# Three edits to a decoder trunk: Gate normalized by ScalarE, paired k tiles in the values' units, one low half earlier

## The chip, the cores and the metric

The kernel runs on one core of one Trainium2 chip. The metric is the device time of one execution in microseconds. Before the change the median of 3 runs is 386.59 us (385.78 to 387.56).

## The reference, cut to what matters

One layer of a decoder trunk. The input x (1024 tokens by 1024 channels) is projected once into all branches; three branches are gated, concatenated and projected out, and a LayerNorm closes the layer. The branch that the change touches is the gating MLP, called Gate here:

```python
z = x @ w_in
u_a, v_a, g_a, x_b, g_b, q_x, g_x = split(z)
# Gate: 4 heads of 128 channels, chunks of 128 tokens
vh    = layer_norm(gelu(v_a) per token and head, ln_g, ln_b)
mixed = einsum('hts,bcshd->bcthd', tril(w_s), vh) + b_s
y_a   = gelu(u_a) * mixed * silu(g_a)
# two more branches: a diagonal state-space layer (y_b), attention into 256 memory tokens (y_x)
y   = concat([y_a, y_b * silu(g_b), y_x * silu(g_x)])
out = layer_norm(2**0.25 * x + y @ w_out, ln_g, ln_b)
```

## The kernel before

Large products are made in three passes: an operand is split into a high half (`h_...`, rounded to the matmul's format by a copy, mostly on ScalarE) and a low half (`l_...`, the rest, a subtraction on VectorE), and TensorE adds high*high, high*low and low*high (`mm3`, L142; `mm3x2`, L148). x itself lies transposed and split in `xh` and `xl`, eight k tiles of 128 input channels.

The program runs through these stages: a first stage (L543 to L563) that streams x and the weights of two branches in and multiplies them as they land; keys and values of the memory (`KV`); then a list of *units* (`run_units`, L176), each of which multiplies 128 or 512 output columns by all of x; then the output projection (L1160 on). A feature unit (`fm`, L181) makes 128 features for all tokens in two PSUM banks. A values' unit (`vu`, L198) makes 512 columns of v for 4 token tiles of 128, in four PSUM banks: `for kt` over six k tiles, inside it `for t` over the four token tiles, and then the last two k tiles token tile by token tile, each followed by its evacuation. There are two such units, v0 (tokens 0 to 511) and v1. The order of units is xb0, xb1, gb0, gb1, v0, u0 to u3, v1, g0 to g3. Weights come in pieces of 128x512; high and low halves have 6 buffers each (`NPC`).

Beside the units run jobs written as generators. `tick(cost)` after some matmuls advances a notional clock, and jobs whose time has come put their next instructions into the program. Two kinds matter here:

- `ssm_batch` (L722), four batches of the state-space layer. Each has a step in which TensorE transposes `L` into PSUM (`pp`), ScalarE copies it to SBUF (`PP`, L755), and TensorE multiplies with it (`up`, L780); VectorE then makes a scan and `H` (L787 to L802), and TensorE uses `H` in `yp` (L808). GpSimd makes the tables C, S and Q for the next batch (L743 to L777).
- `mix_all(th)` (L892), once after each values' unit. VectorE makes the variance column `rsv` (L895), GpSimd raises it to the power -0.5 (L896), then each of 16 tiles of 128x128 in `nv` (4 heads, 4 chunks) is normalized by one VectorE instruction with two per-partition columns, mean and 1/std (L902); TensorE mixes them with the masked matrix `wT` (`mx`, L911) and VectorE scales the result into `ya`.

TensorE's instructions stand in the order in which the program text issues them, through the whole kernel. Between the KV stage and the output projection, `ordered("p")` leaves the order on VectorE, ScalarE and GpSimd to a scheduler, which places each instruction by estimated times; each engine then runs its own list strictly in order. In the first stage and in the output projection the text's order stands on those engines too.

In the first stage, k tile 0 is loaded in cuts. The weight's second half (`i == 1`, L510 to L523) is split by VectorE (cast `h_wgq`, subtraction `l_wgq`), and `xl[:, 0, half[1]]`, the low half of x's second 512 tokens, follows it.

Of the kernel before, what the change touches and what calls it, by code (L numbers as in the profile page):

```python
# [9 lines left out]
F32 = mybir.dt.float32  # L10
# [3 lines left out]
AF = mybir.ActivationFunctionType  # L14
ALU = mybir.AluOpType
# [3 lines left out]
P = 128  # L19
KT = 8  # L20
# [16 lines left out]
def trunk_kernel(ctx, tc, xT, x, w_gq, w_kv, memT, w_fm, w_v, w_o,  # L37
# [3 lines left out]
    V, S, G, T = nc.vector, nc.scalar, nc.gpsimd, nc.tensor  # L41
# [13 lines left out]
    def mul(eng, o, a, b):  # L55
        eng.tensor_tensor(o, a, b, op=ALU.mult)
# [4 lines left out]
    def sub(eng, o, a, b):  # L61
        eng.tensor_tensor(o, a, b, op=ALU.subtract)  # L62

    def split(hi, lo, src):
        S.copy(hi, src)  # L65
        sub(V, lo, src, hi.bitcast(F32))

    def open_pool(name, bufs=1, side="left", space=None):
        st = ExitStack()
        kw = dict(name=name, bufs=bufs)  # L70
        if space is not None:
            kw["space"] = space
        else:
            kw["side"] = side
        return st, st.enter_context(tc.tile_pool(**kw))
# [12 lines left out]
    def zbank(name):  # L88
        return psz.tile([P, 512], F32, tag="z", name=name)

    def ubank(name):
        return psu.tile([P, 512], F32, tag="u", name=name)
# [28 lines left out]
    def tick(cost):  # L121
        now[0] += cost
        advance()
# [6 lines left out]
    def load(src, name, shape=(P, 512), pool=None, tag="raw", bufs=NRAW):  # L130
        raw = (pool or stream).tile(list(shape), F32, tag=tag, bufs=bufs, name=f"r_{name}")
        nc.sync.dma_start(out=raw, in_=src)
        return raw

    def piece(src, name):
        raw = load(src, name)
        hi = stream.tile([P, 512], F32R, tag="hi", bufs=NPC, name=f"h_{name}")
        lo = stream.tile([P, 512], F32R, tag="lo", bufs=NPC, name=f"l_{name}")
        split(hi, lo, raw)
        return hi, lo  # L140

    def mm3(ps, sh, sl, mh, ml, start, stop, chk=False):  # L142
        kw = dict(skip_group_check=True) if chk else {}
        T.matmul(ps, lhsT=sh, rhs=mh, start=start, stop=False, **kw)  # L144
        T.matmul(ps, lhsT=sh, rhs=ml, start=False, stop=False, **kw)  # L145
        T.matmul(ps, lhsT=sl, rhs=mh, start=False, stop=stop, **kw)  # L146
# [9 lines left out]
    xh = xpool.tile([P, KT, SEQ], F32R, name="xh")  # L156
    xl = xpool.tile([P, KT, SEQ], F32R, name="xl")
# [4 lines left out]
    half = [slice(0, 512), slice(512, 1024)]  # L162
# [35 lines left out]
    def vu(h, evac, done):  # L198


        def run(u, nxt):
            ps = [zbank(f"zv{h}{t}") for t in range(4)]

            def mm(t, kt):
                ts = slice((4 * h + t) * P, (4 * h + t) * P + P)
                mm3(ps[t], xh[:, kt, ts], xl[:, kt, ts], *u.pcs[kt], kt == 0, kt == KT - 1)

            for kt in range(KT - 2):
                u.fetch(kt + 4)
                for t in range(4):  # L210
                    mm(t, kt)
                    if t % 2:
                        tick(1.36)
            for t in range(4):
                for kt in (KT - 2, KT - 1):
                    mm(t, kt)
                evac(t, ps[t])
                if t == 3:
                    done()
                tick(1.36)  # L220
                if t in (1, 2) and nxt is not None:
                    nxt.fetch(t)
        return Unit(f"v{h}", lambda i: w_v[:, i], KT, run, 4)
# [275 lines left out]
    def stage(kt):  # L499
        if kt == 0:  # L500
            ws, xs = [], []
            for i, (a, b) in enumerate(cuts):
                ws.append(load(w_gq[:, kt, a:b], f"wgq0{i}", shape=(P, 256)))
                if i == 0:
                    xs = [load(xT[:, kt, c:d], f"x0{c}", shape=(P, 256), pool=mpool, tag="xraw",
                               bufs=NXR) for c, d in cuts]
                    r1 = load(xT[:, kt, half[1]], "x01")
            wt = []
            for i, raw in enumerate(ws):
                wh = stream.tile([P, 256], F32R, tag="hi", bufs=NPC, name=f"h_wgq0{i}")  # L510
                wl = stream.tile([P, 256], F32R, tag="lo", bufs=NPC, name=f"l_wgq0{i}")
                V.tensor_copy(wh, raw)
                if i == 0:
                    for r, (c, d) in zip(xs, cuts):
                        S.copy(xh[:, 0, c:d], r)
                sub(V, wl, raw, wh.bitcast(F32))
                if i == 0:
                    for r, (c, d) in zip(xs, cuts):
                        sub(V, xl[:, 0, c:d], r, xh[:, 0, c:d].bitcast(F32))
                    S.copy(xh[:, 0, half[1]], r1)  # L520
                else:
                    sub(V, xl[:, 0, half[1]], r1, xh[:, 0, half[1]].bitcast(F32))
                wt += [(wh[:, 0:P], wl[:, 0:P]), (wh[:, P:256], wl[:, P:256])]  # L523
        else:
            wh, wl = piece(w_gq[:, kt], f"wgq{kt}")
            for h in range(2):
                split(xh[:, kt, half[h]], xl[:, kt, half[h]],
                      load(xT[:, kt, half[h]], f"x{kt}{h}", pool=mpool, tag="xraw", bufs=NXR))
            wt = [(wh[:, tok[f]], wl[:, tok[f]]) for f in range(4)]
        return wt  # L530

    def first_half(wt):
# [7 lines left out]
        for w, x in ((0, 0), (0, 1), (1, 0)):  # L540
            mm(1, w, x, 0, 512, w + x == 0)

    wts = [stage(0)]  # L543
    for kt in range(KT):
        wt = wts[kt]
        if kt < KT - 1:
            wts.append(stage(kt + 1))
        if kt == KT - 1:
            kv.fetch(1)
        for f in range(4):  # L550
            wh, wl = wt[f]
            if kt == 0 and f < 2:
                if f == 0:
                    first_half(wt)
                mm3(fps[f][1], wh, wl, xh[:, 0, half[1]], xl[:, 0, half[1]], True, False)
            else:
                mm3x2(fps[f], wh, wl, kt, kt == 0, kt == KT - 1,
                      skip=(0,) if f < 2 else ())
            if kt == KT - 1 and f < 2:
                for h in range(2):  # L560
                    S.activation(yx[:, f, half[h]], fps[f][h], AF.Silu)
        if kt < KT - 1:
            tick(5.2)  # L563
# [136 lines left out]
    gb0 = fm(0, "gb0", raw_to(yb, 0))  # L700
    gb1 = fm(1, "gb1", raw_to(yb, 1))
    v_units = [vu(h, lambda t, ps, h=h: v_evac(h, t, ps), lambda h=h: v_done(h)) for h in range(2)]
    run_units([*xb, gb0, gb1], v_units[0])
    drain()
# [7 lines left out]
    gm_st, gm = open_pool("gm", side="right")  # L712
# [176 lines left out]
    def v_done(th):  # L889
        spawn(mix_all(th))  # L890

    def mix_all(th):  # L892
        v = nv[th]
        _, mv, rs = stt[th]
        V.tensor_scalar(rs, mv[:, :, 1], LN_EPS, None, op0=ALU.add)  # L895
        G.tensor_tensor(rs, rs, nhalf, op=ALU.pow)  # L896
        yield 5.0
        for hd in range(4):
            for c in range(4):
                i = c * 4 + hd  # L900
                sl = v[:, c, tok[hd]]
                V.tensor_scalar(sl, sl, mv[:, i, 0:1], rs[:, i:i + 1], op0=ALU.subtract,  # L902
                                op1=ALU.mult)
            yield 1.0
        yield 4.0
        for hd in range(4):
            while hd not in have_u:
                yield 1.0
            ps = ubank(f"mx{hd}{th}")
            for c in range(4):  # L910
                T.matmul(ps[:, tok[c]], lhsT=v[:, c, tok[hd]], rhs=wT[:, hd],  # L911
                         start=(c == 0), stop=(c == 3), skip_group_check=True)
            now[0] += 0.85
            mt = gm.tile([P, 4, P], F32, tag="mt", bufs=2, name=f"mt{hd}{th}")
            V.scalar_tensor_tensor(mt, ps.rearrange("p (c t) -> p c t", c=4),
                                   gmg[:, hd:hd + 1],
                                   tbias[:, hd].unsqueeze(1).to_broadcast([P, 4, P]),
                                   op0=ALU.mult, op1=ALU.add)
            mul(V, ya[:, hd, half[th]], ya[:, hd, half[th]], mt.rearrange("p c t -> p (c t)"))
            yield 2.0  # L920
# [395 lines left out]
```

## Time and profile before

| what | value |
|---|---|
| runs | 386.59 us median of 3 (385.78 to 387.56) |
| the profiled execution | 383.81 us, its span 382.1 us |
| TensorE busy | 367.4 us (96%) |
| VectorE busy | 293.8 us (77%) |
| ScalarE busy | 181.5 us (48%) |
| GpSimd busy | 96.7 us (25%) |
| mean granted TensorE clock | 0.989 |

The profile is of one execution. A timeline row gives start and length in microseconds, the engine (PE is TensorE, DVE VectorE, ACT ScalarE, POOL GpSimd), the line, the operation, the tile written and the tiles read, and in square brackets the time that the engine stood idle just before and what ended it. Ends of matmuls are modelled, so what a stop costs is best read from start to start.

### The profile page before, as it was taken

How to read it: one execution, taken by the hardware profiler on the slowest of the kernel's cores; microseconds unless marked ns; L12 is line 12 of the kernel's file. 1: busy time of each engine (PE TensorE's matmuls, PEld its weight loads, DVE VectorE, ACT ScalarE, POOL GpSimd, SP SyncE). 2: the span in 40 equal slices, each digit the busy share in tenths (PEclk: the TensorE clock that was granted, in tenths of full speed). 3: DMA queues.
4: the chain of work that ended last, by engine and by line, in shares of the span. 5: the costliest groups of instructions: out<-in, count | busy, mean ns of one | idle time of the engine just before them, and what ended most of it. 6: DMA issues, size and time to landing. Idle time of an engine off the chain costs nothing.

```text
span 382.1 us, 5532 instructions
## 1 busy us (share of the span) xinstructions
PE 367.4 (96%) x1877; PEld 310.0 (81%) x1877; DVE 293.8 (77%) x639; ACT 181.5 (48%) x349; POOL 96.7 (25%) x87
## 2 busy tenths in 40 slices
PE   8999999999999999999999999999999999999980
PEld 7888898888888788888888888888888888877870
DVE  4699897988886599969788459775538997777783
ACT  4573597567774635232132334333424667545430
POOL 1305000001000593860873800500000022003541
PEclk9999999999999999999999999999999999999995
DMA  7984436237899776202212232400107959820988
GB/s 221 302 274 124 131 112 192 86 98 206 171 188 235 189 196 162 60 29 58 69 41 60 55 95 62 165 2 0 57 4 214 380 152 225 208 84 0 256 224 235
DMA packets 28628, 53.69 MB, mean 141 GB/s; under 512 B 5928, under 2 KB 9400, under 8 KB 27448
## 3 DMA queue, kind: packets, MB, share of 16 engines
q1 hardware_dynamic: 26296, 44.43, 38.0%
q0 software_dynamic: 2160, 8.39, 11.8%
q10 hardware_dynamic: 144, 0.52, 0.4%
q8 instruction: 15, 0.25, 0.3%
q14 instruction: 13, 0.11, 0.1%
HBM read 44.87 MB, written 13.63 MB: 153 GB/s over the span
## 4 chain that ended last, share of the span: by engine, by line
PE 67%; DVE 19%; issue 4%; ACT 4%; DMA 3%; POOL 1%; SPq 0%; POOLq 0%; DVEq 0%; ACTq 0%
PE zg L151 4%; PE zg L152 4%; PE zg L154 4%; PE zv L144 3%; PE zv L146 3%; PE zv L145 3%; PE av L624 2%; PE zxb L152 2%; PE zxb L154 2%; PE zxb L151 2%; PE q L152 2%; PE q L154 2%; PE q L151 2%; DVE l_u L62 2%; DMA r_wo<-in_w_o_dram 2%
## 5 line engine op out<-in xcount | busy, mean ns | idle before, releaser
L144 PE MATMUL zv<-h_v,xh 128*128 128x512 f32 x64 | 25.6, 400 | 0.3 <-ACT yb L229 0.3
L151 PE MATMUL zu<-xh,h_u 128*128 128x512 f32 x64 | 25.9, 404 | 0.0
L151 PE MATMUL zg<-xh,h_g 128*128 128x512 f32 x64 | 25.5, 398 | 0.0
L152 PE MATMUL zu<-xl,h_u 128*128 128x512 f32 x64 | 25.0, 391 | 0.0
L152 PE MATMUL zg<-xl,h_g 128*128 128x512 f32 x64 | 25.0, 390 | 0.0
L146 PE MATMUL zv<-h_v,xl 128*128 128x512 f32 x64 | 25.0, 390 | 0.0
L145 PE MATMUL zv<-l_v,xh 128*128 128x512 f32 x64 | 24.9, 389 | 0.0
L1029 POOL DMA_DIRECT2D l_wo<-ws_s x6 | 5.2, 863 | 72.8 <-ACT l_wo L1028 66.0
L65 ACT CAST h_v<-r_v 128x512 fp32r<-128x512 f32 x16 | 9.9, 619 | 26.5 <-PE zu L152 18.6
L62 DVE TENSOR_TENSOR l_v<-r_v,h_v 128x512 fp32r<-128x512 f32 x16 | 16.7, 1050 | 6.3 <-ACT h_v L65 6.2
L154 PE MATMUL zu<-xh,l_u 128*128 128x512 f32 x64 | 19.8, 390 | 0.0
L154 PE MATMUL zg<-xh,l_g 128*128 128x512 f32 x64 | 19.7, 390 | 0.0
L596 ACT ACTIVATE pr<-s,nm 128x256 f32<-128x256 f32 x32 | 14.9, 473 | 7.9 <-DVE nm L592 6.5
L1072 POOL TENSOR_TENSOR stat<-stat,nhalf 128x1 f32<-128x1 f32 x7 | 10.3, 1466 | 24.1 <-DVE stat L1071 24.1
L1066 ACT ACTIVATE junk<-res,stat 128x1024 bf16<-128x1024 f32 x7 | 8.1, 1150 | 16.6 <-DVE stat L1062 15.2
L902 DVE TENSOR_SCALAR nv<-nv,mv,rsv 128x128 f32<-128x128 f32 x32 | 13.3, 487 | 3.0 <-POOL rsv L896 3.0
L144 PEld LDWEIGHTS zv<-h_v,xh 128*128 128x128 f32 x64 | 12.0, 188 | 3.0 <-ACT yb L229 0.7
L62 DVE TENSOR_TENSOR l_wo<-r_wo,h_wo 128x512 fp32r<-128x512 f32 x18 | 12.1, 686 | 2.7 <-ACT h_wo L65 2.7
L154 PEld LDWEIGHTS zu<-xh,l_u 128*128 128x128 f32 x64 | 12.0, 188 | 2.6
L146 PEld LDWEIGHTS zv<-h_v,xl 128*128 128x128 f32 x64 | 12.0, 188 | 2.6
L154 PEld LDWEIGHTS zg<-xh,l_g 128*128 128x128 f32 x64 | 12.0, 188 | 2.6
L151 PEld LDWEIGHTS zg<-xh,h_g 128*128 128x128 f32 x64 | 12.0, 188 | 2.3
(371 smaller groups left out, 1187.2 us busy)
## 6 DMA issues: line engine op xcount, KB each, us to landing
r_v<-in_w_v_dram SPq DMA_DIRECT2D x16, 256.0 KB, 2.9
ws_s<-in_w_o_dram SPq DMA_DIRECT2D x4, 1024.0 KB, 6.2
r_wo<-ws_s SPq DMA_DIRECT2D x16, 256.0 KB, 3.4
res<-in_x_dram SPq DMA_DIRECT2D x4, 1024.0 KB, 11.7
r_x<-in_xT_dram SPq DMA_DIRECT2D x15, 256.0 KB, 4.5
r_wo<-in_w_o_dram SPq DMA_DIRECT2D x12, 256.0 KB, 4.4
out_dram<-res SPq DMA_DIRECT2D x6, 512.0 KB, 4.0
res<-lnp POOLq DMA_DIRECT2D x5, 512.0 KB, 4.6
```

The lines of the kernel that those rows point to most:

```text
L62: eng.tensor_tensor(o, a, b, op=ALU.subtract)
L65: S.copy(hi, src)
L144: T.matmul(ps, lhsT=sh, rhs=mh, start=start, stop=False, **kw)
L145: T.matmul(ps, lhsT=sh, rhs=ml, start=False, stop=False, **kw)
L146: T.matmul(ps, lhsT=sl, rhs=mh, start=False, stop=stop, **kw)
L151: T.matmul(ps[h], lhsT=wh, rhs=xh[:, kt, half[h]], start=first, stop=False, **kw[h])
L152: T.matmul(ps[h], lhsT=wh, rhs=xl[:, kt, half[h]], start=False, stop=False, **kw[h])
L154: T.matmul(ps[h], lhsT=wl, rhs=xh[:, kt, half[h]], start=False, stop=last, **kw[h])
L596: S.activation(pr[:, h], ps3[:, h], AF.Exp, bias=nm[:, h:h + 1], scale=1.0, accum_out=rs[:, h:h + 1])
L902: V.tensor_scalar(sl, sl, mv[:, i, 0:1], rs[:, i:i + 1], op0=ALU.subtract, op1=ALU.mult)
L1066: S.activation(junk, res[:, t], AF.Square, bias=nmean[:, i1], scale=1.0, accum_out=ssq[:, i1])
L1072: G.tensor_tensor(rsd[:, i], rsd[:, i], nhalf[:, 0:n], op=ALU.pow)
```

## The change

Three edits. In a values' unit two k tiles are multiplied for token tiles 0 and 1, and then the same two k tiles for token tiles 2 and 3; the calls that fetch pieces and the ticks keep their places. In the first stage `xl[:, 0, half[1]]` is made right after the cast of the weight's second half, ahead of that weight's low half. In `mix_all` VectorE makes one more column, nb = -mean/std, and the 16 tiles are normalized by ScalarE, as Identity(scale * v + nb) with 1/std as the scale, in place of the 16 VectorE instructions.

```diff
     def vu(h, evac, done):
...
-            for kt in range(KT - 2):
-                u.fetch(kt + 4)
-                for t in range(4):
-                    mm(t, kt)
-                    if t % 2:
+            for k0 in range(0, KT - 2, 2):
+                for t0 in (0, 2):
+                    u.fetch(k0 + 4 + t0 // 2)
+                    for kt in (k0, k0 + 1):
+                        for t in (t0, t0 + 1):
+                            mm(t, kt)
                         tick(1.36)
...
                 V.tensor_copy(wh, raw)
+                if i == 1:
+                    sub(V, xl[:, 0, half[1]], r1, xh[:, 0, half[1]].bitcast(F32))
...
-                else:
-                    sub(V, xl[:, 0, half[1]], r1, xh[:, 0, half[1]].bitcast(F32))
...
         G.tensor_tensor(rs, rs, nhalf, op=ALU.pow)
+        nb = gm.tile([P, 16], F32, tag="nbv", name=f"nbv{th}")
+        V.scalar_tensor_tensor(nb, mv[:, :, 0], -1.0, rs, op0=ALU.mult, op1=ALU.mult)
         yield 5.0
         for hd in range(4):
             for c in range(4):
                 i = c * 4 + hd
                 sl = v[:, c, tok[hd]]
-                V.tensor_scalar(sl, sl, mv[:, i, 0:1], rs[:, i:i + 1], op0=ALU.subtract,
-                                op1=ALU.mult)
+                S.activation(sl, sl, AF.Identity, bias=nb[:, i:i + 1], scale=rs[:, i:i + 1])
```

The scheduler gives the instructions these places. On ScalarE, behind v0, before (numbers in names are buffers; `zu` is a u unit's PSUM, `pp` and `up` are the second batch's of `ssm_batch`):

```order
L814 ACTIVATE ytok_1909<-yp_1900 128x4x8x16
L65 CAST h_u_0_2173<-r_u_0_2171 128x512
L755 COPY PP_1984<-pp_1979 128x512
L65 CAST h_u_1_2197<-r_u_1_2195 128x512
L926 ACTIVATE ya<-zu_1886 128x512
L926 ACTIVATE ya<-zu_1887 128x512
L785 COPY ju_2045<-up_2038 64x512
```

and in the change:

```order
L816 ACTIVATE ytok_1911<-yp_1902 128x4x8x16
L65 CAST h_u_0_2175<-r_u_0_2173 128x512
L906 ACTIVATE nv_1810<-nv_1810,nbv_1886,rsv_1813 128x128 x16
L757 COPY PP_1986<-pp_1981 128x512
L65 CAST h_u_1_2199<-r_u_1_2197 128x512
L929 ACTIVATE ya<-zu_1888 128x512
L929 ACTIVATE ya<-zu_1889 128x512
L787 COPY ju_2047<-up_2040 64x512
```

All 16 activations of v0 stand between a cast and the copy of PP, and everything behind them keeps its order. Behind v1 the other 16 stand between two casts of `yth` and the table load ahead of g0's Silu; no table load is added on either place.

On VectorE at the same place, before:

```order
L887 BN_AGGR mv_1812<-stt_1811 128x2 x4
L895 TENSOR_SCALAR rsv_1813<-mv_1812 128x16
L902 TENSOR_SCALAR nv_1810<-nv_1810,mv_1812,rsv_1813 128x128 x16
L62 TENSOR_TENSOR l_u_0_2174<-r_u_0_2171,h_u_0_2173 128x512
L765 COPY K_1991<-kp_1986 128x16 x4
L56 TENSOR_TENSOR L_2153<-Fr,B_145 128x512
```

and in the change:

```order
L889 BN_AGGR mv_1812<-stt_1811 128x2 x4
L897 TENSOR_SCALAR rsv_1813<-mv_1812 128x16
L900 SCALAR_TENSOR_TENSOR nbv_1886<-mv_1812,rsv_1813 128x16
L62 TENSOR_TENSOR l_u_0_2176<-r_u_0_2173,h_u_0_2175 128x512
L767 COPY K_1993<-kp_1988 128x16 x4
L56 TENSOR_TENSOR L_2155<-Fr,B_145 128x512
```

The small nb has the place of the 16. GpSimd's list is the same in both, with Q of the next batch right behind the power.

On VectorE in the batch that leads to the first `yp`, one subtraction `l_u` moves from ahead of `jg` to behind the first product of `H`; before:

```order
L793 SCALAR_TENSOR_TENSOR t_1758<-r_155,v_1757 128x128 x4
L62 TENSOR_TENSOR l_u_0_1935<-r_u_0_1932,h_u_0_1934 128x512
L796 TENSOR_SCALAR jg_1794<-t_1758 64x512
L797 COPY jg_1794<-t_1758 64x512
L56 TENSOR_TENSOR H_1795<-C_1647,t_1758 128x4x127
L56 TENSOR_TENSOR jg_1794<-S_1648,jg_1794 128x512
L62 TENSOR_TENSOR l_u_1_1952<-r_u_1_1949,h_u_1_1951 128x512
L59 TENSOR_TENSOR H_1795<-H_1795,jg_1794 128x4x127
```

and in the change:

```order
L795 SCALAR_TENSOR_TENSOR t_1758<-r_155,v_1757 128x128 x4
L798 TENSOR_SCALAR jg_1794<-t_1758 64x512
L799 COPY jg_1794<-t_1758 64x512
L56 TENSOR_TENSOR H_1795<-C_1647,t_1758 128x4x127
L62 TENSOR_TENSOR l_u_0_1937<-r_u_0_1934,h_u_0_1936 128x512
L56 TENSOR_TENSOR jg_1794<-S_1648,jg_1794 128x512
L62 TENSOR_TENSOR l_u_1_1954<-r_u_1_1951,h_u_1_1953 128x512
L59 TENSOR_TENSOR H_1795<-H_1795,jg_1794 128x4x127
```

As many instructions stand ahead of the last one as before. TensorE's list differs in the two values' units alone.

## Rows read from the trace of the kernel before

**Rows 1.** The page: busy time of each engine.
```profile
PE 367.4 (96%) x1877; PEld 310.0 (81%) x1877; DVE 293.8 (77%) x639; ACT 181.5 (48%) x349; POOL 96.7 (25%) x87
```
**Rows 2.** Timeline of TensorE, its stops and the matmul before three of them.
```profile
7.04 0.50 PE L145 MATMUL gx<-xl,h_wgq 128*128 128x512 f32 x1 [0.47 <-DVE xl L62]
...
129.03 0.39 PE L146 MATMUL zv<-h_v,xl 128*128 128x512 f32 x1
129.75 0.50 PE L144 MATMUL zv<-h_v,xh 128*128 128x512 f32 x1 [0.32 <-ACT yb L229]
...
155.35 0.39 PE L806 MATMUL yp<-M,X 128*128 128x128 f32 x2
156.15 0.46 PE L808 MATMUL yp<-Q,H 128*128 128x128 f32 x2 [0.41 <-DVE H L59]
...
183.72 0.39 PE L806 MATMUL yp<-M,X 128*128 128x128 f32 x2
184.64 0.46 PE L808 MATMUL yp<-Q,H 128*128 128x128 f32 x2 [0.54 <-DVE H L59]
...
342.14 0.50 PE L144 MATMUL o<-h_wo,T4h 128*128 128x512 f32 x1 [0.48 <-DVE res L1101]
```
**Rows 3.** Timeline of VectorE, first stage.
```profile
5.96 0.42 DVE L62 TENSOR_TENSOR l_wgq<-r_wgq,h_wgq 128x256 fp32r<-128x256 f32 x1
6.30 0.68 DVE L62 TENSOR_TENSOR xl<-r_x,xh 128x512 fp32r<-128x512 f32 x1
```
**Rows 4.** Window: length, then PE, PEld, DVE, ACT, POOL busy, PEclk, DMA share, GB/s.
```profile
129.60:162.30 32.70, 32.15 (x158) 26.95 (x159) 32.41 (x66) 13.07 (x22) 24.90 (x20) 1.00 0.59 154
```
**Rows 5.** Timeline of VectorE and GpSimd around both power and K.
```profile
139.95 1.62 POOL L59 TENSOR_TENSOR S<-S,t 128x512 f32<-128x512 f32 x1
140.35 1.30 DVE L59 TENSOR_TENSOR K<-K,ddiag 16x64 f32<-16x64 f32 x1
...
162.36 2.93 POOL L896 TENSOR_TENSOR rsv<-rsv,nhalf 128x16 f32<-128x16 f32 x1 [1.23 <-DVE rsv L895]
165.27 1.05 POOL L56 TENSOR_TENSOR Q<-wr,Cc 128x512 f32<-128x512 f32 x1
165.32 6.95 DVE L902 TENSOR_SCALAR nv<-nv,mv,rsv 128x128 f32<-128x128 f32 x16 [3.04 <-POOL rsv L896]
173.72 0.20 DVE L59 TENSOR_TENSOR K<-K,ddiag 16x64 f32<-16x64 f32 x1
```
**Rows 6.** Timeline of ScalarE and TensorE around PP and up.
```profile
163.95 0.59 ACT L755 COPY PP<-pp 128x512 f32<-128x512 f32 x1 [3.03 <-PE pp L753]
167.62 1.08 ACT L926 ACTIVATE ya<-zu 128x512 f32<-128x512 f32 x2
170.06 1.05 PE L780 MATMUL up<-X,PP 128*128 128x128 f32 x8
```
**Rows 7.** Groups of ScalarE by line and shape: busy us, mean ns, idle before.
```profile
L65 ACT CAST xh<-r_x 128x512 fp32r<-128x512 f32 x14 | 8.6, 620 | 3.2 <-DMA r_x<-in_xT_dram 2.8
L934 ACT ACTIVATE sg<-zg 128x512 f32<-128x512 f32 x8 | 4.4, 596 | 13.2 <-PE zg L154 13.2
L848 ACT ACTIVATE sgl<-gl,glub 128x512 f32<-128x512 f32 x4 | 2.7, 687 | 8.9 <-PE gl L146 8.9
L515 ACT CAST xh<-r_x 128x256 fp32r<-128x256 f32 x2 | 0.8, 405 | 1.5 <-DMA r_x<-in_xT_dram 1.4
```
**Rows 8.** Timeline of ScalarE behind v1.
```profile
249.80 1.09 ACT L934 ACTIVATE sg<-zg 128x512 f32<-128x512 f32 x2 [2.36 <-PE zg L154]
```
**Rows 9.** TensorE's first matmuls and its last; the window behind it, as in rows 4.
```profile
1.09 3.17 PE L243 MATMUL warm<-warm 128*128 128x128 bf16 x28 [1.09 <-DVE warm L240]
...
4.79 0.61 PE L534 MATMUL gx<-xh,l_wgq 128*128 128x256 f32 x2
...
370.67 0.28 PE L146 MATMUL o2last<-yx_wo,B21l 128*128 128x256 f32 x1
...
374.00:378.00 4.00, 0.00 (x0) 0.00 (x0) 1.54 (x3) 0.00 (x0) 0.39 (x1) 0.50 1.02 275
```

## Prediction

> **What bounds the kernel now.** I read the page first, then TensorE's timeline for its stops, then the rows of the engines that end each stop. The page gives TensorE 367.4 us of busy time, 96% of the span [rows 1]: the kernel is bound by TensorE's own list, and a change in another engine counts only where TensorE stops, or is made to stop. The timeline shows few stops [rows 2]. At 7.04 TensorE waits for `xl`, at 129.75 for a PSUM bank that ScalarE empties, at 156.15 and at 184.64 for VectorE's `H`. The one at 342.14 lies in the output projection, follows from work that starts behind the last unit, and has no part in the change. So the most that the three edits can give back is the first four.
>
> Read from start to start, their price is this. Matmuls of 512 columns stand about 0.23 us apart; between 129.03 and 129.75 lie 0.72, so 0.49 are lost, and some 0.1 more while the pipe fills again (the matmul behind the stop takes 0.50, its neighbour 0.39). Between 155.35 and 156.15 lie 0.80 where two matmuls of 128 columns take 0.23 (`up` shows eight in 1.05, with the last one's tail [rows 6]): 0.57 lost. At 183.72 to 184.64 it is 0.92 less 0.23: 0.69 lost [rows 2].
>
> The second thing to see is VectorE between 129.60 and 162.30: busy for 32.41 of 32.70 us [rows 4]. In that stretch VectorE sets the time of `H`, and of the variance column behind it; TensorE arriving earlier does not make them earlier.
>
> **The change part by part.**
>
> *x's low half ahead of the weight's.* VectorE makes `l_wgq` from 5.96 and `xl` from 6.30 to 6.98, and TensorE resumes at 7.04 [rows 2, 3]. With the two exchanged, `xl` starts at 5.96: 0.34 earlier. The weight's low half then starts at about 6.6 and ends at 7.0; it is first read by the third feature tile, which TensorE reaches six matmuls, 1.4 us, after the stop. Everything up to v0 runs behind TensorE, so all of it moves by 0.34, VectorE's full stretch too.
>
> *Two k tiles for two token tiles.* The third and fourth bank of v0 are first written behind four groups of three matmuls, not two: 12 x 0.23 = 2.7 us after the unit's start instead of 1.4. The wait at 129.75 was one third of a microsecond, so it goes, and TensorE gains 0.6. The second k tile's piece is needed 1.4 us earlier; pieces 0 to 3 are fetched during the unit before, so I cost this at nothing. A piece's buffer comes free 1.4 us later for every second k tile; the casts that wait for it belong to pieces at least four k tiles ahead, 4 x 2.7 us of cover. But the gain does not last: 26 us later `H` decides, and it has moved by 0.34 only. The moved `l_u` changes nothing there: the same instructions stand ahead of the last one of `H`. So at 156 the stop grows from 0.57 to some 1.2 us, and the net gain is 0.3.
>
> *The 16 activations behind v0.* This is the term that decides. GpSimd's power ends at 162.36 + 2.93 = 165.29, now 164.99. VectorE's nb reads two SBUF operands, and GpSimd starts Q right behind the power [rows 5]. How such a pair runs is seen at 140.35: K, 16x64 with two inputs, took 1.30 us and ended when GpSimd's S (139.95 + 1.62) ended; the same K with GpSimd at rest took 0.20 [rows 5]. So I let nb end with Q, at 165.27 + 1.05 + 0.1 - 0.3 = 166.1. Bounds: 165.2 if it isn't held; 166.1 as taken.
>
> Then 16 activations of 128x128. No row has one. ScalarE's copies from SBUF take 620 ns for 512 columns and 405 for 256, so 0.84 ns a column, and 297 ns for 128; an activation with a per-partition bias takes 687 where one without takes 596 (both from PSUM), 91 more [rows 7]. Two columns (bias and scale) make 297 + 182 = 479. Neighbours overlap by 0.1: two activations of 0.59 took 1.08 [rows 6]. So 15 x 0.38 + 0.48 = 6.2 us. Bounds: 15 x 0.2 + 0.3 = 3.3 with columns free, 16 x 0.48 = 7.7 without overlap. I take 6.2, since both extra prices are read from this engine. ScalarE ends them at 166.15 + 6.2 = 172.35.
>
> Behind them in ScalarE's list stands the copy of PP, which ran at 163.95 before, 6.1 us ahead of the `up` at 170.06 that reads it [rows 6]. That cover is gone: PP starts at 172.3 and ends at 172.9, `up` starts at 173.0 instead of 170.06. TensorE stands for some 2.9 us, and is 2.9 us late behind it. Also queued behind PP are a cast, u0's evacuation (its banks are needed a unit later) and `ju`, whose delay VectorE can take, as follows.
>
> The Trainium skill (ScalarE: Activation LUTs, Rules for kernel authors) says that adding and multiplying belong on VectorE rather than ScalarE. By that rule alone the block would be longer than VectorE's; here VectorE took 6.95 us for the same 16 [rows 5], so by length the move costs nothing, and the loss that I forecast is one of place.
>
> *VectorE without its 16.* It loses 6.95 us behind v0 and gains nb, 0.2 to 1.1. Between the power and the second `yp` VectorE had been full; now it waits for `ju` (some 2.9 us late, with TensorE) and has 3 us to spare. The stop at 184.64 goes: 0.69 back.
>
> *The 16 behind v1.* There ScalarE had been idle for 2.36 us ahead of g0's Silu [rows 8]; 6.2 us more delay that Silu by some 4. Its two banks are wanted again by g2, one unit (48 x 0.23 = 11 us) later. `mx` needs one head's four tiles at a time. I cost this at nothing.
>
> **The sum.** Net at `up`: +2.9 (the first edit's 0.34 is in it); behind 184: -0.7. That is +2.2. Against the profiled execution: 383.81 + 2.2 = 386.0. That execution lies 2.8 below the median of the runs shown, so the forecast as a median is 386.59 + 2.2 = 388.8 us, 0.6% slower.
>
> **The rivals.**
>
> *A. The block is covered (not slower).* If PP is written by 169.7, TensorE never stops there. It takes nb unheld (-0.9) and activations no slower than 0.23 apart (-2.3). For it: VectorE's list relieved, and an engine with 48% load [rows 1]. Against it: the prices of rows 7. Then only gains are left, 0.3 + 0.7: 385.6.
>
> *B. nb is not held by GpSimd.* Against it stands K at 140.35; for it, that the operands are 16 columns. The stop shrinks by 0.9: 387.9.
>
> *C. The granted clock falls in the stop.* TensorE's last matmul ends at 370.95, and the window from 374.00 has a clock of 0.50, 1.2 GHz, against 1.00 before: a pause of some 3 us was enough there [rows 9]. At the start TensorE ran at that level from 1.09 at least until 4.8 (28 matmuls of 128 columns 0.11 apart; 256 columns 0.2 apart [rows 9]), so a fall costs about half of 3.7 us: 388.8 + 1.9 = 390.7. The forecast stop is 2.9, on the edge; against it, shorter stops left the clock at 1.00 [rows 4]. The Trainium skill (TensorE: Matmul & The Clock Gate, Part 1) says that the slow clock is the default and returns after idle time; the tail agrees.
>
> *D. All four stops go and no new one comes:* 0.34 + 0.6 + 0.57 + 0.69 = 2.2 back, 384.4. It needs `H` to be earlier at 156, which full VectorE speaks against.
>
> **How the numbers follow.** Forecast 0.52, A 0.13, B 0.15, C 0.14, D 0.06. The forecast alone spreads over 387.6 to 390.2 (the block's price and the runs' scatter). About 0.5%, 1.93 us, is what a measurement of this kernel can tell from no change: slower begins at 388.52, faster below 384.66. Two thirds of the forecast and all of C are slower, with a little of B: 0.50. D is faster: 0.06. The rest, 0.44, lies between. For 8 in 10 the range leaves out D, the lower half of A and the upper end of C: 385.6 to 391.0.
>
> **What would show it.** Right: TensorE's stop at 7 near 0.1, none at the start of v0, a longer one at the first `yp`, a new one of 2 to 3 us ahead of `up` ended by ScalarE's PP, none at the second `yp`. VectorE some 12 us less busy, ScalarE about 12 more. Wrong: PP done before `up` (A), nb of 0.2 us next to a busy GpSimd (B), a clock below 1.00 between 170 and 180 (C), or a stop behind v1.

## The result: 388.69 us against 386.18, and the profile after

| what | before | after |
|---|---|---|
| median of 20 runs each | 386.18 us (384.84 to 388.24) | 388.69 us (386.36 to 391.67) |
| ratio, 95% interval | | 1.0064 [1.0046, 1.0082] |
| the profiled execution, its span | 383.81, 382.1 us | 387.51, 385.8 us |

The change makes the kernel 0.64% slower. The forecast was 388.8 us, with slower as the likeliest side. Here and below a ratio and its interval come from the runs within 1.5% of a kernel's fastest, so a ratio need not be the quotient of the two medians beside it. Line numbers behind the first edits are higher by 2 to 4 than in [rows 1 to 9].

The page's row of busy times, after:

```profile
PE 366.6 (95%) x1877; PEld 310.3 (80%) x1877; DVE 285.3 (74%) x609; ACT 193.8 (50%) x381; POOL 97.1 (25%) x87
```

Against [rows 1] VectorE is 8.5 us less busy, where some 12 was forecast, and ScalarE 12.3 more, as forecast; TensorE has the same work. TensorE's timeline, after, shows where it stands now; the columns are those of [rows 2]:

```profile
7.45 0.50 PE L145 MATMUL gx<-xl,h_wgq 128*128 128x512 f32 x1 [0.18 <-DVE xl L62]
...
133.53 0.39 PE L146 MATMUL zv<-h_v,xl 128*128 128x512 f32 x1
135.41 0.63 PE L755 MATMUL pp<-ident,L 128*128 128x128 f32 x4 [1.49 <-issue]
...
158.66 0.46 PE L810 MATMUL yp<-Q,H 128*128 128x128 f32 x2 [1.51 <-DVE H L59]
...
175.59 1.16 PE L782 MATMUL up<-X,PP 128*128 128x128 f32 x8 [2.85 <-ACT PP L757]
...
189.53 0.39 PE L810 MATMUL yp<-Q,H 128*128 128x128 f32 x2
...
346.14 0.50 PE L144 MATMUL o<-h_wo,T4h 128*128 128x512 f32 x1 [0.68 <-DVE res L1104]
```

Against [rows 2]: the stop in v0 at 129.75 is gone, and so is the second yp's. The first yp's grew from 0.41 to 1.51. Two are new: 2.85 us ahead of `up`, ended by PP as forecast, and 1.49 us ahead of `pp`, which the prediction does not have. From start to start TensorE is, against before, 0.42 late where v0 starts, 1.42 at `pp`, 2.52 behind the first yp, 5.53 at the second batch's `up`, 4.81 behind the second yp, and 3.72 at the end. The medians differ by 2.5; the two profiles differ by 1.2 more. The stop ahead of `pp` can account for about 1 of that: before's profiled execution has none, and the experiments show that it belongs to none of the edits.

The 1.1 that TensorE wins back between the second yp and the end is in no term of the prediction. Most of it lies in the output projection. Its matmuls with `T1`, the first and the last of 48, before and then after:

```profile
302.92 0.40 PE L144 MATMUL o<-h_wo,T1h 128*128 128x512 f32 x1
...
313.89 0.39 PE L146 MATMUL o<-h_wo,T1l 128*128 128x512 f32 x1
```
```profile
307.22 0.39 PE L144 MATMUL o<-h_wo,T1h 128*128 128x512 f32 x1
...
317.87 0.39 PE L146 MATMUL o<-h_wo,T1l 128*128 128x512 f32 x1
```

They take 10.97 us before and 10.65 after, at a granted clock of 1.00 in both. The same two times, to a hundredth, stand in the profiles of all the experiments below: counting these two, 10.97 in each of the six kernels in which VectorE normalizes the 16 tiles, 10.65 in each of the eight in which ScalarE does. Over the projection's 336 matmuls (231 against 228 ns apart, stops left out) that is about 1.2 us in favour of the ScalarE edit. Why is open: the edit also adds a tile, nb, so other tiles may lie elsewhere in memory, and no run tests that.

The timelines of VectorE, GpSimd and ScalarE, after, around the new stop ahead of `up`:

```profile
164.71 2.92 POOL L898 TENSOR_TENSOR rsv<-rsv,nhalf 128x16 f32<-128x16 f32 x1 [2.77 <-DVE rsv L897]
167.62 1.05 POOL L56 TENSOR_TENSOR Q<-wr,Cc 128x512 f32<-128x512 f32 x1
```
```profile
167.67 1.03 DVE L900 SCALAR_TENSOR_TENSOR nbv<-mv,rsv 128x16 f32<-128x16 f32 x1 [3.04 <-POOL rsv L898]
...
249.56 0.19 DVE L900 SCALAR_TENSOR_TENSOR nbv<-mv,rsv 128x16 f32<-128x16 f32 x1
```
```profile
168.80 6.27 ACT L906 ACTIVATE nv<-nv,nbv,rsv 128x128 f32<-128x128 f32 x16 [5.40 <-DVE nbv L900]
174.98 0.56 ACT L757 COPY PP<-pp 128x512 f32<-128x512 f32 x1
175.44 0.61 ACT L65 CAST h_u<-r_u 128x512 fp32r<-128x512 f32 x1
175.96 1.06 ACT L929 ACTIVATE ya<-zu 128x512 f32<-128x512 f32 x2
177.05 0.58 ACT L787 COPY ju<-up 64x512 f32<-64x512 f32 x1
```

The chain is the one forecast: power, nb until Q's end, 16 activations in 6.27 us, PP, `up`. nb of v0 takes 1.03 us beside Q, nb of v1 0.19 with GpSimd at rest.

**A correction to the part on the change.** It says that GpSimd's list is the same in both. It is not: the paired k tiles also move one instruction there. In the batch behind the first `H`, the subtraction C<-C,t now stands ahead of the product S<-sn,cn. (Further on they also exchange a cast and an activation on ScalarE and a few instructions on VectorE.) Before, in GpSimd's list, and then its timeline after:

```order
L56 TENSOR_TENSOR C_1916<-cn 128x512
L56 TENSOR_TENSOR S_1917<-sn,cn 128x512
L62 TENSOR_TENSOR C_1916<-C_1916,t_1918 128x512
```
```profile
153.34 1.45 POOL L56 TENSOR_TENSOR C<-cn 128x512 f32<-128x512 f32 x1 [1.53 <-DVE H L56]
154.87 1.62 POOL L62 TENSOR_TENSOR C<-C,t 128x512 f32<-128x512 f32 x1
156.46 1.51 POOL L56 TENSOR_TENSOR S<-sn,cn 128x512 f32<-128x512 f32 x1
```

E6 below puts that back alone.

### The profile page after: what moved, and what is told of

Read it like the earlier page. It is cut to its first block, busy times and chain, and to the rows that moved or that the text cites. A ratio compares the mean times of both kernels' runs of the same rounds, so it can differ in the third digit from the quotient of the medians.

```text
span 385.8 us, 5534 instructions
## 1 busy us (share of the span) xinstructions
PE 366.6 (95%) x1877; PEld 310.3 (80%) x1877; DVE 285.3 (74%) x609; ACT 193.8 (50%) x381; POOL 97.1 (25%) x87
## 4 chain that ended last, share of the span: by engine, by line
PE 71%; DVE 13%; ACT 5%; DMA 4%; issue 3%; POOL 1%; SPq 0%; POOLq 0%; DVEq 0%; ACTq 0%
PE zg L151 4%; PE zg L152 4%; PE zg L154 4%; PE zv L146 3%; PE zv L144 3%; PE zv L145 3%; PE zu L151 3%; PE zu L152 3%; PE zu L154 3%; PE av L626 2%; PE zgb L154 2%; PE zgb L152 2%; PE zxb L152 2%; PE zxb L154 2%; PE zgb L151 2%
## 5 line engine op out<-in xcount | busy, mean ns | idle before, releaser
L62 DVE TENSOR_TENSOR l_v<-r_v,h_v 128x512 fp32r<-128x512 f32 x16 | 15.9, 998 | 10.7 <-ACT h_v L65 10.6
L56 DVE TENSOR_TENSOR ya<-ya,sg 128x512 f32<-128x512 f32 x8 | 5.2, 687 | 15.7 <-ACT sg L937 15.7
L906 ACT ACTIVATE nv<-nv,nbv,rsv 128x128 f32<-128x128 f32 x32 | 12.5, 480 | 5.4 <-DVE nbv L900 5.4
L65 ACT CAST h_wo<-r_wo 128x512 fp32r<-128x512 f32 x18 | 10.9, 618 | 6.2 <-DMA r_wo<-ws_s 4.1
```

Of the source, the lines that this page charges most:

```text
L906: S.activation(sl, sl, AF.Identity, bias=nb[:, i:i + 1], scale=rs[:, i:i + 1])
```

## Experiments

Each ratio is against runs of the kernel before on the same chip, taken beside them. E1 to e4 ran on one chip, e5 to e8 on a second, e9 to e12 on a third, so differences between these groups are less sure than those within one.

**One part at a time (e1 to e4).** E1 is the third hunk alone (x's low half), e2 the first hunk alone (paired k tiles), e3 the last hunk alone (ScalarE and nb), e4 the first two edits without ScalarE:

E1, and e4 with e2's lines:

```diff
+                if i == 1:
+                    sub(V, xl[:, 0, half[1]], r1, xh[:, 0, half[1]].bitcast(F32))
...
-                else:
-                    sub(V, xl[:, 0, half[1]], r1, xh[:, 0, half[1]].bitcast(F32))
```

> Only x's low half is made ahead of the weight's; everything else as before. By the forecast's step TensorE's stop near 7 us shrinks from 0.47 to about 0.1, every milestone up to the last stop before the output projection moves by 0.34, and the time falls by 0.3 (about 386 us where before is 386.3). Rival: it gives nothing, since the weight's second half, whose cast stands ahead of both, lands when it lands, and a stop of some 0.2 to 0.5 us stays; time unchanged, and nothing to see beyond the scatter of the landing.

E2:

```diff
-            for kt in range(KT - 2):
...
+            for k0 in range(0, KT - 2, 2):
+                for t0 in (0, 2):
...
```

> Only the paired k tiles in the values' units, with the places that the scheduler then gives (one subtraction of a weight's low half moved on VectorE, GpSimd's C minus t ahead of the product S). By the forecast's step the stop at v0's third bank goes (0.6 gained), and the gain is lost again at the first yp, whose H is not earlier: time unchanged, within 0.3. Theory formed from the trace of the change: with GpSimd's list in the new order three instead of two of VectorE's operations there are held by GpSimd's, H is about 0.9 later than the shorter lead allows, the stop at the first yp is 1.4 to 1.6, and the time is 0.3 to 0.9 longer than before. Rival: the gain is kept, 0.6 shorter.

E3:

```diff
+        V.scalar_tensor_tensor(nb, mv[:, :, 0], -1.0, rs, op0=ALU.mult, op1=ALU.mult)
...
-                V.tensor_scalar(sl, sl, mv[:, i, 0:1], rs[:, i:i + 1], op0=ALU.subtract,
-                                op1=ALU.mult)
+                S.activation(sl, sl, AF.Identity, bias=nb[:, i:i + 1], scale=rs[:, i:i + 1])
```

> Only the 16 tiles moved to ScalarE, with nb. Theory (place): the copy of PP behind the 16 makes a stop ahead of up of 2.9 to 3.2 us, the second yp stop (0.7) goes, time 2.2 to 2.6 longer than before (1.006 to 1.007). Rival (the block's extra instructions or the clock cost everywhere): the stop at up is under 2, and the rest of the loss lies elsewhere. Rival (most of the loss of the whole change comes from the first two edits): under 1 us longer.

> The first two edits without the third. Theory: no stop at up; stop near 7 us smaller, none at v0's third bank, 1.4 to 1.6 at the first yp; the time is within 0.6 of before, and 2 to 3 below the whole change. Rival (what the whole change loses it loses before up): 1 us or more slower than before.

| kernel | median (range, runs) | ratio, 95% interval |
|---|---|---|
| before | 385.56 (382.65 to 389.14, 31) | |
| e1, x's low half | 385.75 (384.08 to 388.33, 12) | 1.0017 [0.9989, 1.0046] |
| e2, paired k tiles | 386.42 (382.73 to 388.16, 12) | 1.0023 [0.9993, 1.0054] |
| e3, ScalarE | 389.21 (387.24 to 390.61, 8) | 1.009 [1.0054, 1.0125] |
| e4, e1 and e2 | 387.32 (382.37 to 388.06, 12) | 1.0027 [0.9994, 1.0061] |

The ScalarE edit alone is slower by as much as the whole change or more: 3.6 us, where 2.2 to 2.6 was expected. The other two, alone or together, can't be told from before; e4's interval leaves room for a loss of 2.4 us. E3's stops on TensorE's timeline:

```profile
136.02 0.63 PE L753 MATMUL pp<-ident,L 128*128 128x128 f32 x4 [2.00 <-issue]
...
158.16 0.46 PE L808 MATMUL yp<-Q,H 128*128 128x128 f32 x2 [0.41 <-DVE H L59]
...
175.26 1.16 PE L780 MATMUL up<-X,PP 128*128 128x128 f32 x8 [2.99 <-ACT PP L755]
```

The stop of 2.9 to 3.2 ahead of `up` is there, and the rival that saw most of the loss in the first two edits falls. Behind that stop the granted clock, 1.00 before it, fell to 0.50, which is 1.2 GHz, and TensorE lost another 1.7 us from start to start before it was back at 1.00. The same happened in e6 below, where it lost 1.5. E3's window, then e6's, columns as in [rows 4]:

```profile
177.00:180.00 3.00, 3.00 (x13) 2.63 (x12) 1.29 (x2) 0.90 (x2) 0.00 (x0) 0.50 0.35 98
```
```profile
176.00:179.00 3.00, 3.00 (x10) 2.42 (x10) 1.29 (x2) 1.36 (x3) 0.00 (x0) 0.50 0.40 108
```

That is rival C of the prediction. How many of e3's 8 runs have it is not shown, nor how much it adds to their 3.6 us.

E3 also has a stop of 2.00 ahead of `pp`, though it changes nothing ahead of that place. E2 has one of 2.21, e4 of 1.85, e1 of 0.32, before none. So this stop belongs to none of the edits. At the first yp e4 has the 1.49 that was expected; e2 has none, because its clock fell to 0.50 behind the stop ahead of `pp` and TensorE came 1.5 later. In every one of these profiles VectorE's first product for `L` waits for the same thing, a transfer of 32 bytes from `ot` (L636, L666). VectorE's timeline, of before, of after and of e3, and GpSimd's of before:

```profile
129.62 0.69 DVE L56 TENSOR_TENSOR L<-Fr,B 128x512 f32<-128x512 f32 x1 [2.15 <-DMA ws_s<-ot]
```
```profile
127.45 0.42 DVE L56 TENSOR_TENSOR yx<-yx,ot 128x256 f32<-128x256 f32 x1
131.05 0.69 DVE L56 TENSOR_TENSOR L<-Fr,B 128x512 f32<-128x512 f32 x1 [3.17 <-DMA ws_s<-ot]
```
```profile
131.67 0.69 DVE L56 TENSOR_TENSOR L<-Fr,B 128x512 f32<-128x512 f32 x1 [4.29 <-DMA ws_s<-ot]
```
```profile
129.63 0.99 POOL L719 MEMSET M<- 128x512 f32 x2 [2.83 <-DMA ws_s<-ot]
```

`L` reads nothing of that transfer, and the memset of `M`, which waits for it too, reads nothing at all. If they wait all the same, the reason is likely to be memory: both belong to a pool opened (L713) behind the closing of the attention stage's pool (L705), and may lie where `ot` lies, which the transfer still reads. E7 tests whether the reading of `ot` is what they wait for.

**One instruction moved (e5, e6).** E5 is the whole change with the second batch's PP copied by VectorE; e6 is the whole change with GpSimd's S back ahead of C minus t in that batch. In both, the lists of all engines are otherwise as in the change:

```diff
-        S.copy(PP, pps.rearrange("p (g q) -> p g q", g=NG))
+        (V.tensor_copy if bi in (1,) else S.copy)(PP, pps.rearrange("p (g q) -> p g q", g=NG))
```

```diff
+            sm = G.tensor_tensor(v4(Sn), sa, cb, op=ALU.mult)
+            with tc.issue_after(sm.ins):
+                sub(G, C, C, t1)
```

> The whole change, but the second batch's copy of PP is VectorE's instead of ScalarE's: one instruction leaves its place behind the 16 activations, all else keeps its order. Theory (the loss is one of place): the stop ahead of up goes or falls under 0.3, since VectorE has nothing to do there; of the 2.85 us some part may return at the second yp, because ju still stands behind the 16 on ScalarE: time 2 to 2.9 below the whole change, 386 to 386.7. Rival (length: whatever waits for ScalarE's block waits all the same): the stop moves on to the second yp with 2 us or more, time 388 or above. Rival (the loss was made ahead of up, by the late L and the first yp): time unchanged.

> The whole change, with GpSimd's product S put back ahead of its subtraction C minus t, as before. Theory (GpSimd's new order holds three of VectorE's operations ahead of the first H instead of two): jg, l_u and H are held twice, not three times, H ends about 0.5 to 1.0 earlier against pp, and the stop at the first yp falls from 1.5 to 0.5 to 1.0, the time by as much. Rival (the stop at the first yp is set by when L is ready and by what VectorE has to do, not by the order on GpSimd): 1.4 to 1.6 again, or whatever the wait ahead of pp leaves of it; time unchanged.

| kernel | median (range, runs) | ratio, 95% interval |
|---|---|---|
| before | 385.58 (382.23 to 388.25, 22) | |
| e5, PP on VectorE | 385.58 (384.69 to 388.0, 12) | 1.0019 [0.9992, 1.0045] |
| e6, S ahead of C minus t | 388.52 (387.57 to 390.18, 10) | 1.0074 [1.0045, 1.0102] |

E5's block on ScalarE is as long as in after, and TensorE passes `up` without a stop:

```profile
167.66 6.28 ACT L905 ACTIVATE nv<-nv,nbv,rsv 128x128 f32<-128x128 f32 x16 [3.75 <-DVE nbv L899]
```
```profile
168.09 0.68 DVE L756 COPY PP<-pp 128x512 f32<-128x512 f32 x1
```
```profile
173.09 1.05 PE L781 MATMUL up<-X,PP 128*128 128x128 f32 x8
```

One copy taken out from behind the block takes the loss back, as far as this can be measured: e5 is 2.9 us below e6, which ran beside it and takes as long as the whole change, and its interval holds before's time. No second yp stop returns, though `ju` still runs behind the block. The loss is one of place, not of length.

E6's time can't be told from the whole change's (1.0074 and 1.0064), where 0.5 to 1.0 less was expected. Its rows at the first yp can; VectorE's timeline, first of after, then of e6:

```profile
153.78 1.56 DVE L56 TENSOR_TENSOR jg<-S,jg 128x512 f32<-128x512 f32 x1
155.27 1.77 DVE L62 TENSOR_TENSOR l_u<-r_u,h_u 128x512 fp32r<-128x512 f32 x1
156.96 1.55 DVE L59 TENSOR_TENSOR H<-H,jg 128x508 f32<-128x508 f32 x1
```
```profile
153.81 1.57 DVE L56 TENSOR_TENSOR jg<-S,jg 128x512 f32<-128x512 f32 x1
155.30 0.68 DVE L62 TENSOR_TENSOR l_u<-r_u,h_u 128x512 fp32r<-128x512 f32 x1
155.90 1.56 DVE L59 TENSOR_TENSOR H<-H,jg 128x508 f32<-128x508 f32 x1
```
And e6's stops on TensorE's timeline:

```profile
135.45 0.63 PE L760 MATMUL pp<-ident,L 128*128 128x128 f32 x4 [2.29 <-issue]
...
157.60 0.46 PE L815 MATMUL yp<-Q,H 128*128 128x128 f32 x2 [0.44 <-DVE H L59]
```

With the old order on GpSimd `l_u` takes 0.68 instead of 1.77, `H` ends 1.1 sooner behind the same `L`, and the stop is 0.44 instead of 1.51. The stop ahead of `pp` is 0.8 longer than in after's profile only because TensorE comes there 0.8 earlier. Behind the first yp e6's TensorE is 1.06 ahead of after's; the fall of the clock behind `up`, shown above, turns that into 0.7 behind. So the 1.1 is shown at its place and not in the time. The Trainium skill (SBUF — State Buffer, SBUF: two separate sides) says that of a VectorE operation with two SBUF inputs and a GpSimd operation that reads SBUF, the one that starts first locks the other out for a whole instruction; 0.68 against 1.77 us agrees.

**The wait ahead of L (e7).** The kernel before, with the 32 bytes read from `yx`, which stays, instead of `ot`. The bytes are overwritten by the next copy; they only make it wait.

```diff
+            last_yx[0] = yx[0:1, hp, lq * 256:lq * 256 + 8]
...
-        sum_copy("s3", quarter["a21"], last_ot[-1])
+        sum_copy("s3", quarter["a21"], last_yx[0])
```

> The kernel before, with one transfer changed: the 32 bytes that are sent ahead of the last copy of w_o are read from yx and not from ot. Theory (L waits for no data, but for the memory that this small transfer still reads, which lands 2.9 us after its issue in the profile of before and 4.0 to 5.1 in those of the change and of the third edit alone): L starts at about 127.5 instead of 129.6 to 131.7, no stop ahead of pp, and the two yp stops shrink or go (1.3 together); with the 0 to 2 us that pp costs in other runs, 1.5 to 2.5 us faster than before (0.994 to 0.996). Rival (L's memory is held by something else as well, or VectorE's load alone sets H): L at its old place or the yp stops as they were, time unchanged.

Measured: 382.34 us (382.08 to 383.77, 7 runs) against 385.58, ratio 0.9918 [0.9888, 0.9949]. SyncE's timeline of e7, and VectorE's:

```profile
127.36 0.25 SPq L667 DMA_DIRECT2D ws_s<-yx  x1
132.57 0.50 SPq L668 DMA_DIRECT2D ws_s<-in_w_o_dram  x1
```
```profile
127.44 0.69 DVE L56 TENSOR_TENSOR L<-Fr,B 128x512 f32<-128x512 f32 x1
```

The transfer lands as late as ever, 5.2 us after its issue, but `L` starts at 127.44. So the reading of `ot` held it; that they share memory is the likely reason and is not shown by an address. No stop is left at `pp` or either yp. E7 gains 3.2 us, where 1.5 to 2.5 was expected and the profile of before has only 1.3 us of yp stops to give, and its 7 runs lie within 1.7 us where the 22 of before lie within 6. This fits a before that is as late as e2's or e3's profile in most of its runs and was early in the profiled one; such a stop can cost more than its length, as the fallen clock of e2 shows. Each kernel has one profile, so how often is not shown.

What makes the transfer late was not tried, but the same 32 bytes are sent four times in every kernel, and the landings differ with the load on the DMA engines. In before the first, at 82.56, landed within 1.1 us of its issue, while the DMA engines were idle (share 0.00); the third, at 107.17, behind a 1 MB copy on SyncE's own queue, took 6.6 (share 1.01); the fourth, 0.6 us behind a 1 MB transfer that GpSimd issued at 125.98, took 2.9 (share 0.76). In all 14 profiles the first landed within 1.1 us, and the fourth landed before GpSimd's 1 MB did (129.51 against 133.70 in before), so it did not wait for the whole of that. The Trainium skill (DMA: Bandwidth & Descriptors, Queues, rings and completion order) says that a transfer's completion lands only after every earlier write of that DMA engine, across its queues; these landings do not contradict it, and no run here shows it.

**The parts on that quiet base, and a kernel that beats both (e8 to e12).** E9 is e7 with the third edit, e10 e7 with the paired k tiles, e11 e7 with the whole change, e8 e11 with e5's copy, e12 e8 with e6's order. The edits are those shown.

> The whole change with both mends: the second PP copied by VectorE, and the 32 bytes read from yx. Theory: no stop ahead of pp and none ahead of up, the yp stops gone or under 0.3, VectorE with time to spare; only the stops of the first stage and of the output projection stay. 382.5 to 383.5, that is about 3 below before and 5 to 6 below the whole change. Rival (the 16 activations delay ju, and with it the second H): a second yp stop of 1 us or more, time about that of e7 or above it.

> e7 with the third edit alone. Theory (place): in e7's profile the power ends at 163.3 and GpSimd's Q at 164.4; 15 x 0.385 + 0.48 behind that end at 170.7, PP at 171.3, and up, which stood at 169.2, starts at 171.4: a stop of about 2.2, no yp stop to give back, 384.5. Rival (ScalarE's block costs by its length only, or VectorE's freed 7 us pay for it): 382.3 or less.

> e7 with the paired k tiles alone. Theory: the stop at v0's third bank goes (0.6), TensorE reaches the first yp 0.6 earlier, H is 1.1 later because GpSimd's new order holds one more of VectorE's operations, and a stop of 0.5 to 0.6 appears there: 382.3, no change against e7. Rival (the gain is kept): 381.7. Rival (more is lost than gained): 382.8 or more.

> The whole change on e7's base. Theory: e8 with the stop ahead of up back: the power ends at 165.0, the block at 172.4, PP at 173.0, up at 173.0 where e8 has 169.9: 3.1 more than e8, 385.0, and 1.007 of e7. Rival (the whole change owed its loss to the late L): 382 to 383.

> e8 with GpSimd's S put back ahead of C minus t, as in e6. Theory: one held operation less ahead of the first H (1.1 us), so e8's stop of 0.49 at the first yp goes, and the time falls by 0.5 to 381.4, the least of all: e7 less v0's 0.6 and the first stage's 0.3. Rival (H is set otherwise, or the 0.5 is lost again at the second yp, where ju stands behind the 16): 381.9 as e8.

| kernel | median (range, runs) | ratio, 95% interval |
|---|---|---|
| before (beside e9 to e12) | 385.38 (381.74 to 388.1, 29) | |
| e9, e7 and ScalarE | 384.31 (382.68 to 387.29, 12) | 0.9968 [0.9932, 1.0003] |
| e10, e7 and paired k tiles | 383.08 (381.88 to 384.13, 12) | 0.9963 [0.9933, 0.9993] |
| e11, e7 and the whole change | 385.17 (383.42 to 387.05, 12) | 0.9993 [0.9955, 1.0031] |
| e8, e11 and PP on VectorE | 381.93 (381.66 to 383.84, 6) | 0.9904 [0.987, 0.9939] |
| e12, e8 and GpSimd's old order | 381.07 (380.63 to 381.4, 6) | 0.9889 [0.9841, 0.9937] |

Without the late `L` the change costs 385.17 - 382.34 = 2.8 us (2.9 by the two ratios to before), as e11's theory has it, and it is again the stop ahead of `up`; e11's on TensorE's timeline:

```profile
155.84 0.46 PE L810 MATMUL yp<-Q,H 128*128 128x128 f32 x2 [0.79 <-DVE H L59]
...
172.77 1.16 PE L782 MATMUL up<-X,PP 128*128 128x128 f32 x8 [2.85 <-ACT PP L757]
```

E9 came out at 384.3 where 384.5 was expected, though its stop at `up` is 1.59 and not the expected 2.2, since TensorE came 1.1 later from the first stage. E10's theory missed its place. TensorE gained 0.5 in v0 and kept it past the first yp, where `H` was ready in time at 154.95, 0.5 later behind its `L` than in e7 and not 1.1; it lost it at the second yp, a stop that e7 does not have:

```profile
183.43 0.46 PE L810 MATMUL yp<-Q,H 128*128 128x128 f32 x2 [0.36 <-DVE H L59]
```

So with VectorE still making the 16 tiles the pairing gains nothing that can be seen (383.08 against 382.34, on two chips). E8 is 0.4 below e7, which its runs can't tell from no difference, and e12 1.3. What e12 has over e7 is for the most part not the pairing: from its profile's first to last matmul of `o` it takes 76.5 us and e7 77.7, the 1.2 us of the result's section that go with ScalarE's 16 tiles. From v0 to that projection it wins some 0.8. E8 came out under its 382.5 to 383.5, with a stop of 0.49 at the first yp where under 0.3 was expected; the same 1.2 us, which its theory did not have, cover that. E12, in which GpSimd's old order takes that stop away, came out at 381.07 against 381.4. E12 on TensorE's timeline has no stop from v0 to the output projection:

```profile
154.88 0.39 PE L816 MATMUL yp<-Q,H 128*128 128x128 f32 x2
...
168.72 1.05 PE L788 MATMUL up<-X,PP 128*128 128x128 f32 x8
...
182.55 0.39 PE L816 MATMUL yp<-Q,H 128*128 128x128 f32 x2
```

E12 beats both kernels: 1.1% under before. Most of it (3.2 of 4.3 us) is what e7 gives alone.

## Why the prediction was right, and which of its terms were not

**The 16 activations behind v0: right in mechanism and size.** The forecast had nb held until Q's end (1.03 us, Q's 1.05), activations 0.38 apart and 0.48 long (0.385 and 0.478), a block of 6.2 (6.27), and a stop of 2.9 (2.85 in after and e11, 2.99 in e3, 3.07 in e6). E5 shows that it is the copy's place that costs. The Trainium skill (ScalarE: Activation LUTs, Rules for kernel authors) puts adding and multiplying on VectorE. Tile for tile the trace agrees: 13 of VectorE's 16 in before took 0.34 us and stand 0.26 apart. The block as a whole does not follow, 6.27 against 6.95 us ([rows 5]), because VectorE's first three tiles, beside GpSimd, took 1.1 to 1.4 each. E8 and e12, which keep the block on ScalarE, are the fastest kernels, so at this place the move is worth having once nothing urgent stands behind it.

**The second yp: right.** Its 0.7 came back, although `ju` started at 177.05 instead of 171.2.

**Behind v1: right.** The Silu moved from 249.80 to 258.46, some 4 more than TensorE is late there, and TensorE has no stop.

**The first yp: a step that failed.** "The moved `l_u` changes nothing there: the same instructions stand ahead of the last one of `H`" was true of VectorE's list and not of the time. It took the step's length for fixed, while GpSimd's list had changed as well. From L's start to H's end are 26.4 us in before (129.62 to 156.00) and 27.5 in after (131.05 to 158.51); over all 14 profiles 26.3 to 26.6 in the seven kernels with GpSimd's old order, 27.1 to 28.2 in the seven with the new one. So the stretch's length has a term of about +1.1, and not 0. From start to start the stop was forecast to grow by 0.6 all the same, because TensorE would come earlier; from `pp` to the first yp TensorE takes 1.1 more, and for another reason.

**What stood unseen ahead of it.** The prediction took H's time from VectorE being full. What starts that full stretch is `L`, and L's start is set by a transfer whose wait stands in VectorE's rows, 2.15 us in before, and was not read. In after the transfer landed 1.0 us later behind its issue, with the same list ahead of it. So what was won at v0 was lost at `pp` already.

**x's low half: right in mechanism, too small to find.** From the start of the cast `h_wgq` to TensorE's restart are 1.41 us in before (5.63 to 7.04) and 0.95 in after (6.50 to 7.45), so the exchange is worth 0.46 where TensorE waits. But the weight landed 0.87 later in after's execution, and TensorE restarted 0.41 later. In e1's profile the weight landed early and TensorE has no stop there. The 0.34 of the sum is below what one such landing moves.

**The rivals.** A falls (PP was not written in time). B falls with the 1.03 us of nb. C did not come true in the profiled execution: the windows of after with the stop, columns as in [rows 4], show the clock at full speed, 2.4 GHz, in and behind it.

```profile
170.00:175.00 5.00, 2.75 (x13) 1.93 (x11) 3.31 (x4) 5.00 (x15) 1.87 (x2) 1.00 0.19 57
175.00:180.00 5.00, 4.41 (x27) 3.96 (x28) 2.42 (x4) 3.22 (x8) 0.00 (x0) 1.00 0.30 77
```

But C can't be called false. In e3 and e6, behind stops of 2.99 and 3.07 at the same place, the clock did fall, and cost 1.7 and 1.5 us where C reckoned 1.9. And the mean granted clock of the runs points to more of them. In e11, which has the stop and no late `L`, the six runs at 0.979 to 0.987 took 385.24 to 387.05 us, the six at 0.990 to 0.992 took 383.42 to 385.09. Of after's 20 runs, 14 lie at 0.979 to 0.987, with a median of 389.17 us, and six at 0.990 to 0.991, with 388.25. So forecast and C look less like two outcomes of which one holds than like two kinds of execution of one kernel. The mean clock alone doesn't say where in a run it fell, so their shares are not shown.

D falls with the new stop.

**The number.** That +2.2 met a measured +2.5 is luck in part. The terms of the block and of the second yp, 2.9 and -0.7, are right. Four others were not in the sum or were wrong: some 1.1 us for the longer stretch ahead of the first yp and, in part of the runs, a clock at 0.50 behind the stop make after slower; the output projection's 1.2 us make it faster; and the lateness of `L`, which differs from one execution to the next, is in both kernels. That they nearly cancel is not something the prediction foresaw.

## What to carry to other kernels

When work moves to an idle engine, look at what stands behind it in that engine's list: a 0.6 us copy with 6 us of cover was worth 3 us once a block of 6 stood ahead of it, and moving the copy alone took the loss back. Compare the lists of all engines, not only of those the edit names, since a scheduler moves others. Look at more than one profile before a sum is called right: the clock and one transfer made executions of the same kernel differ by more than the change does. And follow a full engine back to what starts its full stretch: here a transfer of 32 bytes that nobody needs held back `L`, and cost about as much as the three edits together.

## What the runs showed of the hardware that was not expected

- 32 bytes from SBUF to DRAM landed within 1.1 us of their issue while the DMA engines were idle, and 2.9 to 5.5 us after it, in the 14 profiles, behind a 1 MB transfer of GpSimd's. Where `L` waited for them the runs of before spread over 6 us; without that wait, over 1.7 (e7, 7 runs) and 0.8 (e12, 6 runs). The runs of e9 and e11, with the stop ahead of `up`, still spread over 4.6 and 3.6; in e11 they fall into two groups by the mean granted clock.
- A stop in the middle of TensorE's work can halve the clock behind it, and need not. The granted clock fell to 0.50 for some 3 us behind stops of 1.87 (e5, first yp), 2.21 (e2, `pp`), 2.99 (e3, `up`) and 3.07 us (e6, `up`), at a cost of 1.5 to 1.7 us each. It stayed at 1.00 behind 2.00 (e3, `pp`), 2.29 (e6, `pp`) and twice 2.85 us (after and e11, `up`). The stop's length alone does not decide it.
- The same 48 matmuls with `T1` took 10.97 us in six kernels and 10.65 in eight others, at the same granted clock of 1.00; what sets the two apart is open.
- A VectorE operation on 16 columns took 0.19 us alone and 1.03 beside one GpSimd operation; one on 512 columns 0.68 and 1.77. What it costs depends on the neighbour more than on its size.
